# Group-query attention: the score products that only serve the row maxima, computed from the high parts alone and two heads at a time

## The chip, the cores and the metric

One core of a Trainium2 chip runs the whole program. The metric is the device time of one execution in microseconds (us); lower is better. A comparison of this kernel with itself settles at about 0.3%, some 5 us.

## What is computed

Two layers of a transformer trunk over 1024 latent and 256 context tokens. The change lies in the first layer, in its group-query attention (GQA): eight query heads of width 64 share two key and value heads. Cut to what matters:

```python
qb = rms_norm(qb.reshape(bsz, t, GQA_HEADS, GQA_HEAD_DIM), q_norm_b)      # 8 heads of 64
kb = rms_norm(kb.reshape(bsz, t, GQA_KV_HEADS, GQA_HEAD_DIM), k_norm_b)   # 2 heads of 64
qb = apply_axial_rope(qb, rope_b); kb = apply_axial_rope(kb, rope_b)      # latents only
sc = jnp.einsum('bqhgd,bkhd->bhgqk', qblk, k) * scale                     # over context + latent keys
p = jax.nn.softmax(sc, axis=-1)
ob = jnp.einsum('bhgqk,bkhd->bqhgd', p, v)
```

Beside GQA the layer has eight heads of latent attention (MLA) with products of 96 rows, which run after the GQA heads through the same code. The second layer is recurrent and not touched.

## The kernel before

Every fp32 operand is split into a high part, rounded to the fast fp32r type, and a low part, the remainder. A query vector q is stored as high and low rows of one 128-row tile (`qh`: rows 0 to 63 high, 64 to 127 low); for keys the tile `kh` has the high part in both halves, and `kl` has the low part and rows of ones.

Attention is cut into 16 units: 8 of GQA (`kind` "g"), then 8 of MLA. A unit is two heads (`j` = 0, 1) and either 768 queries (512 latents and the 256 context tokens) or the other 512 latents. A unit's softmax needs, ahead of its scores, the largest score of every query. `prep_max` makes these: for each head, each tile of 128 queries and each stretch of keys (512, 512, 256) a product with the query tile as weights goes to one PSUM bank (`ps`), and VectorE reduces it to a maximum (`mx`). For GQA this product contracts all 128 rows, (high + low of q) times high of k. The maxima, negated and as two bf16 terms (`nb`), are transposed by four small products against an identity (`bias`, `identbf` in the rows) and copied by ScalarE into two spare rows of `ql`, so that the second score product subtracts them.

`scores` then makes, for each block of 128 keys, two products per head (`pb` tiles, the second with 66 rows of `ql`), and ScalarE takes the exponential. `values` multiplies by v, with the two heads in the two column halves of the array (`pv`). An iteration of the main loop is one block of keys: scores of head 0, a call of `between`, scores of head 1, another `between`; the products of `values` follow every second iteration. `between` advances the preparation of the next unit by `pace` pieces, a piece being one step of `prep_max`. The orders of TensorE and VectorE in this loop are those of the program text; ScalarE's is the scheduler's. Units 0 and 1 are prepared earlier, during the projections, where four pieces are taken at each step, and where products for the modulation (`modw`, four in four column quarters) are interleaved too. In the attention loop the PSUM tag `ps` has 4 banks, `pb` 3 and `pv` 1; during the projections `ps` has all 8.

`post_q` lays out the query tiles that `prep_q_gqa` later loads into `qh` and `ql`. All matrix and elementwise calls go through helpers, so the profile shows line 88 for all of them; tiles tell them apart.

Of the kernel before, what the change touches and what calls it, by code (L numbers as in the profile page):

```python
# [17 lines left out]
P = 128  # L18
# [93 lines left out]
class Trunk:  # L112
# [202 lines left out]
    def project0(self, er, el, att):  # L315
        tc, nc, I, d = self.tc, self.nc, self.I, self.d
# [170 lines left out]
        for c, (t0, n) in enumerate(CH):  # L487
            rk = self.til(wk1, [P, 4, 128], F32, "rawA")
            for i in range(n // P):
                t = t0 // P + i  # L490
# [8 lines left out]
        def post_q(t, acc):  # L499
            raw4 = acc.rearrange("p (t h e) -> p t h e", t=1, e=64)  # L500
            qn = self.norm_rope(wk, raw4, raw4, 1, 8, rope_q, t, "g")[:, 0]
            q2 = self.til(wk, [P, 8, 2, 64], F32R, "q2", bufs=3)
            nc.scalar.activation(q2[:, :, 0], qn, AF.Copy)
            nc.vector.tensor_tensor(q2[:, :, 1], qn, q2[:, :, 0], op=ALU.subtract)

            def pe():
                for g in range(2):
                    qo = self.til(wk, [P, 4, P], F32R, "qo", bufs=3)
                    pq = self.ps([P, 4, P])
                    for j in range(4):  # L510
                        self.tr(pq[:, j], q2[:, 4 * g + j].rearrange("p a b -> p (a b)").bitcast(F32))
                    nc.scalar.activation(qo, pq, AF.Copy)
                    nc.sync.dma_start(d["q12"][t, :, 4 * g:4 * g + 4], qo.bitcast(F32))

            self.defer(3, pe)
# [78 lines left out]
    def attention(self, es):  # L594
# [81 lines left out]
        def prep_q_gqa(u):  # L676
            q_tiles(u)
            p = u["p"]
            a = u["base"] // P
            n = sum(x[1] for x in u["segs"])  # L680
            for j in range(2):
                src = d["q12"][a:a + n // P, :, 2 * p + j, :].rearrange("t p n -> p t n")
                nc.sync.dma_start(u["qh"].bitcast(F32)[:, j, :n].rearrange("p (t n) -> p t n", n=P), src)
                nc.sync.dma_start(u["ql"].bitcast(F32)[0:64, j, :n].rearrange("p (t n) -> p t n", n=P), src[0:64])
            u["k"] = [gk[p // 2], gk[p // 2]]
            yield

# [45 lines left out]

        def prep_max(u):

            K, r0 = (P, 64) if u["kind"] == "g" else (96, 96)
            mt = u["ql"] if u["kind"] == "g" else u["qh"]
            mx = self.til(u0, [P, 8, 3], F32, "mx", bufs=2)
            m8 = self.til(u0, [P, 2, 6, 2], F32, "m8", bufs=2)
# [9 lines left out]
            for t0, n in u["segs"]:  # L749
                if t0 == 0:  # L750
                    yield "late"
                ksegs = [(0, 256)] if t0 == 0 else [(0, 512), (512, 512), (1024, 256)]
                o = (t0 - u["base"]) // P
                nt = n // P
                for j in range(2):
                    kh = u["k"][j][0]
                    for i in range(nt):
                        for g, (s0, sn) in enumerate(ksegs):
                            sp = self.ps([P, 512])
                            self.mm(sp[:, :sn], u["qh"][0:K, j, (o + i) * P:(o + i + 1) * P], kh[0:K, s0:s0 + sn], True, True)  # L760
                            dst = m8[:, j, o + i, 0:1] if t0 == 0 else mx[:, 4 * j + i, g:g + 1]
                            nc.vector.tensor_reduce(dst, sp[:, :sn], axis=AX.X, op=ALU.max, negate=t0 == 0)
                            yield 0
                            if t0 and j and (i, g) == (1, 2):
                                bias(0, t0, n)
                    oo = slice(o, o + nt)
                    red = nc.vector.tensor_reduce
                    if t0:
                        red(m8[:, j, oo, 0], mx[:, 4 * j:4 * j + 4], axis=AX.X, op=ALU.max, negate=True)
                    red(nb[:, j, oo, 0], m8[:, j, oo, 0:1], axis=AX.X, op=ALU.max)  # L770
                    red(m8[:, j, oo, 1], nb[:, j, oo, 0:1], axis=AX.X, op=ALU.max, negate=True)
                    with self.tc.nc.allow_low_precision(reason="the second of two bf16 terms of a maximum"):
                        red(nb[:, j, oo, 1], m8[:, j, oo], axis=AX.X, op=ALU.add)
                yield 3
                if t0 == 0:
                    bias(0, t0, n)
                bias(1, t0, n)

# [196 lines left out]
        for i, it in enumerate(its):  # L975
            ui = it["ui"]
            if ui != cur:
                cur = ui
                if ui + 1 < len(units):
                    nu = units[ui + 1]  # L980
                    if nu["kind"] == "m" and side:
                        for _ in side[0]:
                            pass
                        side = []
                    gens.append([nu["gen"], 0, False])
                    pieces = 25 + (0 if nu["kind"] == "g" else 5 if nu["base"] == 0 else 1)
                    pace = pieces / 14.0 if nu["base"] == 0 else (pieces + 4) / 16.0
            if it["last"] and ui + 1 < len(units):
                while gens and not gens[0][2]:
                    advance(gens[0], True)  # L990
# [1250 lines left out]
```

## Time and profile before

| | before |
|---|---|
| median of 3 runs | 1787.96 us (1785.87 to 1790.78) |
| the profiled execution, its time | 1786.52 us |
| the profiled execution, its span | 1784.7 us |
| TensorE busy | 1630.5 us, 91% |
| VectorE busy | 1177.7 us, 66% |
| ScalarE busy | 741.0 us, 42% |
| GpSimd busy | 811.2 us, 45% |
| granted TensorE clock, mean | 0.96 |

The span is that of the recorded instructions; 1.8 us of the execution lie around it. The GQA units run from about 355 to 612 us of the span, the MLA units after them to about 920 us, and the projections, with the preparation of units 0 and 1, before them.

### The profile page before, as it was taken

To read this page: it belongs to the slowest core of one execution; us is meant where nothing else is said; L and a number is where in the kernel's file an instruction comes from. 1 tells how busy PE (TensorE), PEld (TensorE's weight loads), DVE (VectorE), ACT (ScalarE), POOL (GpSimd) and SP (SyncE) were. 2 spreads that over 40 slices of the span, in tenths; PEclk is the share of its full clock that TensorE was granted. 3 is DMA by queue.
4 is the path that set the end of the run, shared out by engine and by line. 5 is a ranking of instruction groups with operands and counts; after the bars stand their busy time and mean duration, and the time that the engine had idled before them with its cause. 6 is when DMAs were issued, how large, how long until landed. Compare 5 with 4: busy or idle time off the path is not lost.

```text
span 1784.7 us, 25505 instructions
## 1 busy us (share of the span) xinstructions
PE 1630.5 (91%) x9020; PEld 1195.9 (67%) x9020; DVE 1177.7 (66%) x2186; ACT 741.0 (42%) x1500; POOL 811.2 (45%) x727
## 2 busy tenths in 40 slices
PE   5999899989999999999899989988978995898996
PEld 2997766735555566666457876666856883798885
DVE  2657623247566857667847975889956894477787
ACT  2543401145545454444524344767643421233431
POOL 1432200067666678767643851332213794572131
PEclk9999999999999999999999999989989997899998
DMA  9243485164322101121333323333458538985543
GB/s 354 75 154 109 147 292 201 60 142 144 94 53 59 35 22 47 30 59 48 98 98 113 130 91 102 111 107 115 145 140 213 159 115 233 295 259 174 172 147 106
DMA packets 239931, 234.31 MB, mean 131 GB/s; under 512 B 61958, under 2 KB 188306, under 8 KB 237756
## 3 DMA queue, kind: packets, MB, share of 16 engines
q1 hardware_dynamic: 239804, 232.69, 42.8%
q8 instruction: 71, 1.16, 0.3%
q14 instruction: 56, 0.46, 0.1%
HBM read 162.97 MB, written 69.66 MB: 130 GB/s over the span
## 4 chain that ended last, share of the span: by engine, by line
PE 51%; DVE 18%; DMA 13%; issue 7%; ACT 6%; POOL 3%; SPq 2%; ACTq 0%; DVEq 0%; POOLq 0%
PE ps L88 34%; PE pb L88 10%; PE pv L88 7%; DMA wst<-in_att_w_in 2%; DVE f L88 2%; DMA wh<-in_rec_w_out 2%; DVE x L88 2%; DVE yc L88 2%; DVE lw L88 1%; DVE mx L88 1%; DMA qh<-d_q 1%; DMA d_xa<-WX 1%; DVE WX L88 1%; DVE r L88 1%; DVE lu L88 1%
## 5 line engine op out<-in xcount | busy, mean ns | idle before, releaser
L88 DVE TENSOR_REDUCE mx<-ps 128x1 f32<-128x512 f32 (+1 forms) x384 | 207.2, 593 | 155.8 <-PE ps L88 154.1
L88 POOL TENSOR_TENSOR accp<-accp,pt 128x512 f32<-128x512 f32 x202 | 266.0, 1338 | 62.0 <-ACT pt L88 60.4
L88 PE MATMUL ps<-h1h,wf 128*128 128x512 f32 (+1 forms) x864 | 270.5, 388 | 3.5 <-DVE tm L88 1.6
L88 ACT ACTIVATE pt<-pb 128x512 f32<-128x512 f32 (+1 forms) x352 | 194.2, 577 | 185.7 <-PE pb L88 178.0
L88 PE MATMUL pb<-qh,kb 96*128 96x512 f32 (+4 forms) x528 | 210.0, 412 | 5.2 <-ACT pt L88 4.6
L88 PEld LDWEIGHTS ps<-h1h,wf 128*128 128x128 f32 x864 | 161.1, 194 | 35.4 <-issue 3.7
L88 PE MATMUL ps<-h1l,wf 128*128 128x512 f32 (+1 forms) x432 | 163.7, 379 | 0.0
L88 PEld LDWEIGHTS pb<-qh,kb 128*128 128x128 f32 (+2 forms) x528 | 100.1, 191 | 92.6 <-issue 65.4
L88 PE MATMUL pb<-ql,kb 66*128 66x512 f32 (+3 forms) x352 | 137.5, 392 | 0.7 <-ACT ql L88 0.7
L88 PE MATMUL ps<-kb,qh 128*128 128x512 f32 (+3 forms) x416 | 121.7, 368 | 8.9 <-DVE mx L88 5.0
L88 POOL TENSOR_TENSOR accp<-pt,pt 128x512 f32<-128x512 f32 (+1 forms) x47 | 55.9, 1208 | 137.0 <-ACT pt L88 125.3
L88 PEld LDWEIGHTS ps<-kb,qh 128*128 128x128 f32 (+1 forms) x416 | 76.9, 191 | 44.8 <-DVE mx L88 12.8
L88 POOL TENSOR_TENSOR ml<-m,mh 128x512 fp32r<-128x512 f32 (+1 forms) x24 | 52.6, 2205 | 114.0 <-ACT mh L88 114.0
L88 DVE SCALAR_TENSOR_TENSOR yc<-xb,rT,yc 128x1283 f32<-128x1283 f32 (+1 forms) x48 | 84.1, 1759 | 24.5 <-ACT yc L88 24.1
L88 PEld LDWEIGHTS ps<-h1l,wf 128*128 128x128 f32 x432 | 83.9, 194 | 16.6 <-issue 3.6
L88 PE MATMUL ps<-w,mh 128*128 128x512 f32 x256 | 82.5, 404 | 3.4 <-ACT mh L88 3.4
L88 PE MATMUL pv<-pt,vm 128*64 128x512 f32 (+1 forms) x352 | 83.1, 586 | 1.6 <-DVE mo L88 1.6
L88 PE MATMUL pv<-pt,vgqa 128*64 128x512 f32 (+1 forms) x352 | 83.1, 593 | 1.0 <-DVE mo L88 1.0
L88 PE MATMUL ps<-wo,mh 128*128 128x512 f32 x256 | 82.1, 399 | 1.2 <-ACT mh L88 0.7
L88 PE MATMUL ps<-wh,hh 128*128 128x416 f32 (+2 forms) x240 | 82.8, 349 | 0.2 <-ACT hs L88 0.2
L88 PE MATMUL ps<-wh,hl 128*128 128x416 f32 (+2 forms) x240 | 81.7, 343 | 0.0
L88 PE MATMUL ps<-wl,hh 128*128 128x416 f32 (+2 forms) x240 | 81.5, 342 | 0.0
(373 smaller groups left out, 3706.0 us busy)
## 6 DMA issues: line engine op xcount, KB each, us to landing
modw<-in_mod_w SPq DMA_DIRECT2D x16, 1024.0 KB
wfs<-in_rec_w_in SPq DMA_DIRECT2D x22, 512.0 KB
modw<-in_mod_w SPq DMA_DIRECT2D x16, 512.0 KB
wst<-in_att_w_in SPq DMA_DIRECT2D x24, 256.0 KB
d_q<-qo SPq DMA_DIRECT2D x20, 256.0 KB
lx<-d_xl SPq DMA_DIRECT2D x8, 640.0 KB
d_w<-WX SPq DMA_DIRECT2D x20, 256.0 KB
W<-d_w SPq DMA_DIRECT2D x20, 256.0 KB
```

The source lines that it names most:

```text
L88: return fn(*args, **kw)
```

## The change

Three things. First, the layout: for odd heads `post_q` now stores low rows above and high rows below, so that the high parts of head 0 lie in rows 0 to 63 and those of head 1 in rows 64 to 127 of a unit's `qh`; the `ql` load follows this. Second, for GQA `prep_max` contracts only 64 rows (high of q times high of k), and one piece makes the products of both heads, in the two row halves of the array, into two `ps` banks, followed by two reductions. The maximum is thus taken over slightly different scores; it is only the shift of the softmax and cancels in the result. Third, what depends on the pieces: a GQA unit counts 13 pieces instead of 25, with paces of 13/15 and 15/18 of a piece per `between` instead of 25/14 and 29/16, and the two `bias` groups of a segment both come at its end, where before the first came in the middle of head 1. MLA keeps its order.

```diff
-            nc.scalar.activation(q2[:, :, 0], qn, AF.Copy)
-            nc.vector.tensor_tensor(q2[:, :, 1], qn, q2[:, :, 0], op=ALU.subtract)
+            qp, q4 = qn.rearrange("p (g e) n -> p g e n", e=2), q2.rearrange("p (g e) a n -> p g (e a) n", e=2)
+            nc.scalar.activation(q4[:, :, 0::3], qp, AF.Copy)
+            nc.vector.tensor_tensor(q4[:, :, 1:3], qp, q4[:, :, 0::3], op=ALU.subtract)
...
-                nc.sync.dma_start(u["ql"].bitcast(F32)[0:64, j, :n].rearrange("p (t n) -> p t n", n=P), src[0:64])
+                nc.sync.dma_start(u["ql"].bitcast(F32)[0:64, j, :n].rearrange("p (t n) -> p t n", n=P), src[64 * j:64 * j + 64])
...
-                for j in range(2):
-                    kh = u["k"][j][0]
+                pair = u["kind"] == "g"
+                for js in ((0, 1),) if pair else ((0,), (1,)):
                     for i in range(nt):
                         for g, (s0, sn) in enumerate(ksegs):
-                            sp = self.ps([P, 512])
-                            self.mm(sp[:, :sn], u["qh"][0:K, j, (o + i) * P:(o + i + 1) * P], kh[0:K, s0:s0 + sn], True, True)
-                            dst = m8[:, j, o + i, 0:1] if t0 == 0 else mx[:, 4 * j + i, g:g + 1]
-                            nc.vector.tensor_reduce(dst, sp[:, :sn], axis=AX.X, op=ALU.max, negate=t0 == 0)
+                            sps = [self.ps([P, 512]) for _ in js]
+                            for j, sp in zip(js, sps):
+                                r = slice(64 * j, 64 * j + 64) if pair else slice(0, 96)
+                                self.mm(sp[:, :sn], u["qh"][r, j, (o + i) * P:(o + i + 1) * P], u["k"][j][0][r, s0:s0 + sn], True, True)
+                            for j, sp in zip(js, sps):
+                                dst = m8[:, j, o + i, 0:1] if t0 == 0 else mx[:, 4 * j + i, g:g + 1]
+                                red(dst, sp[:, :sn], axis=AX.X, op=ALU.max, negate=t0 == 0)
                             yield 0
-                            if t0 and j and (i, g) == (1, 2):
+                            if t0 and js == (1,) and (i, g) == (1, 2):
                                 bias(0, t0, n)
...
                 yield 3
-                if t0 == 0:
+                if t0 == 0 or pair:
                     bias(0, t0, n)
                 bias(1, t0, n)
...
-                    pieces = 25 + (0 if nu["kind"] == "g" else 5 if nu["base"] == 0 else 1)
-                    pace = pieces / 14.0 if nu["base"] == 0 else (pieces + 4) / 16.0
+                    pieces = 13 if nu["kind"] == "g" else 25 + ( 5 if nu["base"] == 0 else 1)
+                    if nu["base"] == 0:
+                        pace = pieces / (15.0 if nu["kind"] == "g" else 14.0)
+                    else:
+                        pace = (pieces + (2 if nu["kind"] == "g" else 4)) / (18.0 if nu["kind"] == "g" else 16.0)
```

How the order moves, at three places. First TensorE in the middle of a GQA unit, where `pb` are scores of the running unit, `ps<-kb,qh` products for the maxima of the next one, and the last numbers partitions and columns of the output. Before:

```order
L88 MATMUL pb_4534<-qh_4157,kb_3304 128x512
L88 MATMUL pb_4534<-ql_4158,kb_3306 128x512
L88 MATMUL ps_4539<-kb_3304,qh_4482 128x512
L88 MATMUL ps_4542<-kb_3304,qh_4482 128x256
L88 MATMUL pb_4545<-qh_4157,kb_3304 128x512
L88 MATMUL pb_4545<-ql_4158,kb_3306 128x512
L88 MATMUL ps_4550<-kb_3304,qh_4482 128x512
L88 MATMUL ps_4553<-kb_3304,qh_4482 128x512
```

and now:

```order
L88 MATMUL pb_4609<-qh_4157,kb_3304 128x512
L88 MATMUL pb_4609<-ql_4158,kb_3306 128x512
L88 MATMUL ps_4614<-kb_3304,qh_4495 128x512
L88 MATMUL ps_4615<-kb_3304,qh_4495 128x512
L88 MATMUL pb_4620<-qh_4157,kb_3304 128x512
L88 MATMUL pb_4620<-ql_4158,kb_3306 128x512
L88 MATMUL pv_4513<-pt_4543,vgqa_102 64x512
L88 MATMUL pv_4513<-pt_4557,vgqa_102 64x512
```

Two consecutive `ps` products were two pieces of one head; now they are one pair, one in rows 0 to 63 and one in rows 64 to 127, between score products that use all rows. In the GQA loop there are 78 pairs: 61 (40 of 512 columns, 21 of 256) stand between products in the full 128 by 128 shape, 17 (8 of 512, 9 of 256) have `values` products behind them.

Second, TensorE and ScalarE where a new unit begins (its tiles are `qh_4157` and `ql_4158`). TensorE before:

```order
L88 LDWEIGHTS nb_4177
L88 MATMUL ps_4428<-identbf_83,nb_4177 2x128
L88 MATMUL pb_4434<-qh_4157,kb_3304 128x512
L88 MATMUL pb_4434<-ql_4158,kb_3306 128x512
L88 MATMUL ps_4439<-kb_3304,qh_4157 128x256
L88 MATMUL ps_4442<-kb_3304,qh_4157 128x256
L88 MATMUL pb_4445<-qh_4157,kb_3304 128x512
L88 MATMUL pb_4445<-ql_4158,kb_3306 128x512
```

and now:

```order
L88 LDWEIGHTS nb_4182
L88 MATMUL ps_4422<-identbf_83,nb_4182 2x128
L88 LDWEIGHTS nb_4182
L88 MATMUL ps_4428<-identbf_83,nb_4182 2x128
L88 LDWEIGHTS nb_4182
L88 MATMUL ps_4428<-identbf_83,nb_4182 2x128
L88 LDWEIGHTS nb_4182
L88 MATMUL ps_4428<-identbf_83,nb_4182 2x128
L88 LDWEIGHTS nb_4182
L88 MATMUL ps_4428<-identbf_83,nb_4182 2x128
L88 MATMUL pb_4434<-qh_4157,kb_3304 128x512
L88 MATMUL pb_4434<-ql_4158,kb_3306 128x512
```

ScalarE there before:

```order
L88 ACTIVATE ql_4158<-ps_4354 2x512
L88 ACTIVATE pt_4369<-pb_4366 128x512
L88 ACTIVATE pt_4387<-pb_4384 128x512
L88 ACTIVATE pt_4398<-pb_4395 128x512
L88 COPY vm_4100<-ps_4405 128x512
L88 ACTIVATE pt_4419<-pb_4416 128x512
L88 ACTIVATE pt_4424<-pb_4421 128x512
L88 ACTIVATE ql_4158<-ps_4428 2x512
L88 ACTIVATE pt_4437<-pb_4434 128x512
```

and now:

```order
L88 ACTIVATE pt_4405<-pb_4402 128x512
L88 ACTIVATE pt_4418<-pb_4415 128x512
L88 ACTIVATE ql_4158<-ps_4422 2x512
L88 ACTIVATE ql_4158<-ps_4428 2x512
L88 ACTIVATE pt_4437<-pb_4434 128x512
```

The bias of head 0 (`ps_4354`) was copied six ScalarE instructions ahead of that of head 1; now both copies stand right ahead of the unit's first scores, and eight small products stand in a row where four stood. This is so at all six borders between GQA units whose preparation runs in the loop.

Third, TensorE in the projections, at the preparation of unit 1. Before, `modw` products came four in a row:

```order
L88 MATMUL ps_2802<-modw_2857,scT_78 32x512 x4
L88 MATMUL ps_3012<-kb_2300,qh_2868 128x512
L88 MATMUL ps_3015<-kb_2300,qh_2868 128x256
L88 MATMUL ps_3022<-kb_2300,qh_2868 128x512
L88 MATMUL ps_3025<-kb_2300,qh_2868 128x512
```

and now:

```order
L88 MATMUL ps_2882<-modw_2826,scT_78 32x512 x2
L88 MATMUL ps_2897<-kb_2300,qh_2678 128x512
L88 MATMUL ps_2902<-kb_2300,qh_2678 128x512
L88 MATMUL ps_2882<-modw_2826,scT_78 32x512 x2
L88 MATMUL ps_2903<-kb_2300,qh_2678 128x512
```

Four `modw` groups of four stand in eight separate places now, with products for the maxima between, and four of the 26 pairs there (three of 512 columns, one of 256) are themselves parted. Counted over the order, TensorE's shape (rows by columns of the array that a product uses) changes 119 times in the GQA loop before and 248 times now, and 36 and 54 times in the projections.

## Rows read from the trace of the kernel before

**Rows 1.** The page, part 1: busy us, share of the span, instructions.

```profile
PE 1630.5 (91%) x9020; PEld 1195.9 (67%) x9020; DVE 1177.7 (66%) x2186; ACT 741.0 (42%) x1500; POOL 811.2 (45%) x727
```

**Rows 2.** Busy us by stretch: PE, PEld, DVE, ACT, POOL, then PE's clock, DMA share, GB/s.

```profile
233.00:355.00 122.00, 115.47 (x643) 85.93 (x642) 34.31 (x84) 16.10 (x30) 4.14 (x3) 1.00 0.54 177
420.00:460.00 40.00, 39.06 (x177) 21.18 (x175) 29.08 (x58) 21.95 (x42) 29.26 (x24) 1.00 0.29 72
```

**Rows 3.** Waits from 420 to 580 us: who for whom, total us, times, longest.

```profile
DVE mx L88 <- PE ps L88: 36.4, 23, 3.2
...
PE ps L88 <- DVE mx L88: 1.0, 3, 0.6
```

**Rows 4.** Timeline of PE, 377.7 to 384.3 us: start, duration, instruction, count.

```profile
377.79 0.28 PE L88 MATMUL pb<-ql,kb 66*128 66x256 f32 x1
...
378.03 0.29 PE L88 MATMUL pb<-ql,kb 66*128 66x256 f32 x1
...
378.95 0.40 PE L88 MATMUL pb<-ql,kb 66*128 66x512 f32 x1
379.28 1.08 PE L88 MATMUL pv<-pt,vgqa 128*64 128x256 f32 x8
...
382.89 0.40 PE L88 MATMUL pb<-ql,kb 66*128 66x512 f32 x1
...
383.83 0.40 PE L88 MATMUL pb<-ql,kb 66*128 66x512 f32 x1
```

**Rows 5.** Timeline of PE around a product of 16 rows, in the second layer.

```profile
1334.50 0.39 PE L88 MATMUL ps<-maskr,negi 128*128 128x512 f32 x1
1334.82 0.49 PE L88 MATMUL ps<-dec 16*128 16x512 f32 x1
1335.24 0.50 PE L88 MATMUL ps<-h1l,wf 128*128 128x512 f32 x1
1335.58 0.63 PE L88 MATMUL ps<-h1h,wf 128*128 128x512 f32 x2
```

**Rows 6.** PE's timeline and group: fp32 products in rows 0-31 and 32-63 (count | busy, mean ns).

```profile
934.57 0.70 PE L88 MATMUL ps<-grows,sel 32*128 32x512 f32 x2
...
L88 PE MATMUL ps<-grows,sel 32*128 32x512 f32 x4 | 1.1, 640 | 0.0
```

**Rows 7.** Timeline of PE where a new GQA unit begins, from 479 us.

```profile
479.11 0.40 PE L88 MATMUL pb<-ql,kb 66*128 66x512 f32 x1
479.44 0.38 PE L88 MATMUL ps<-identbf,nb 128*2 128x128 bf16 x4
479.76 0.50 PE L88 MATMUL pb<-qh,kb 128*128 128x512 f32 x1
480.10 0.40 PE L88 MATMUL pb<-ql,kb 66*128 66x512 f32 x1
...
480.56 0.39 PE L88 MATMUL pb<-qh,kb 128*128 128x512 f32 x1
480.88 0.50 PE L88 MATMUL pb<-ql,kb 66*128 66x512 f32 x1
```

**Rows 8.** Timeline of ACT there, and at the unit begin near 445 us.

```profile
479.13 1.08 ACT L88 ACTIVATE pt<-pb 128x512 f32<-128x512 f32 x2 [2.01 <-PE pb L88]
480.24 0.59 ACT L88 ACTIVATE ql<-ps 2x512 fp32r<-2x512 f32 x1
...
445.44 0.59 ACT L88 ACTIVATE ql<-ps 2x512 fp32r<-2x512 f32 x1
```

**Rows 9.** Timeline of PE in the projections, around a group of modw products.

```profile
277.75 1.06 PE L88 MATMUL ps<-modw,scT 128*32 128x512 f32 x8
278.74 0.38 PE L88 MATMUL ps<-kb,qh 128*128 128x256 f32 x1
```

**Rows 10.** Groups by form: of 420 to 580 us, then of 140 to 200 us (query layout).

```profile
L88 DVE TENSOR_REDUCE mx<-ps 128x1 f32<-128x512 f32 x80 | 52.5, 681 | 28.3 <-PE ps L88 28.3
...
L88 DVE TENSOR_TENSOR q<-no,q 128x512 fp32r<-128x512 f32 x9 | 6.2, 687 | 4.0 <-ACT q L88 4.0
```

More of the change, by code (lines that the diff above doesn't have):

```diff
@@ L734, in prep_max @@
         def prep_max(u):
-            K, r0 = (P, 64) if u["kind"] == "g" else (96, 96)
+            r0 = 64 if u["kind"] == "g" else 96
             mt = u["ql"] if u["kind"] == "g" else u["qh"]
@@ L754, in prep_max @@
                 nt = n // P
-                for j in range(2):
-                    kh = u["k"][j][0]
+                red = nc.vector.tensor_reduce
+                oo = slice(o, o + nt)
+                pair = u["kind"] == "g"
+                for js in ((0, 1),) if pair else ((0,), (1,)):
                     for i in range(nt):
                         for g, (s0, sn) in enumerate(ksegs):
-                            sp = self.ps([P, 512])
-                            self.mm(sp[:, :sn], u["qh"][0:K, j, (o + i) * P:(o + i + 1) * P], kh[0:K, s0:s0 + sn], True, True)
-                            dst = m8[:, j, o + i, 0:1] if t0 == 0 else mx[:, 4 * j + i, g:g + 1]
-                            nc.vector.tensor_reduce(dst, sp[:, :sn], axis=AX.X, op=ALU.max, negate=t0 == 0)
+                            sps = [self.ps([P, 512]) for _ in js]
[5 more added lines that the diff above has]
+                                red(dst, sp[:, :sn], axis=AX.X, op=ALU.max, negate=t0 == 0)
@@ L763, in prep_max @@
                             yield 0
-                            if t0 and j and (i, g) == (1, 2):
+                            if t0 and js == (1,) and (i, g) == (1, 2):
                                 bias(0, t0, n)
[L766 to L770, printed above, removed]
@@ L771, in prep_max @@
-                    red(m8[:, j, oo, 1], nb[:, j, oo, 0:1], axis=AX.X, op=ALU.max, negate=True)
-                    with self.tc.nc.allow_low_precision(reason="the second of two bf16 terms of a maximum"):
-                        red(nb[:, j, oo, 1], m8[:, j, oo], axis=AX.X, op=ALU.add)
+                    for j in js:
+                        if t0:
+                            red(m8[:, j, oo, 0], mx[:, 4 * j:4 * j + 4], axis=AX.X, op=ALU.max, negate=True)
+                        red(nb[:, j, oo, 0], m8[:, j, oo, 0:1], axis=AX.X, op=ALU.max)
+                        red(m8[:, j, oo, 1], nb[:, j, oo, 0:1], axis=AX.X, op=ALU.max, negate=True)
+                        with self.tc.nc.allow_low_precision(reason="the second of two bf16 terms of a maximum"):
+                            red(nb[:, j, oo, 1], m8[:, j, oo], axis=AX.X, op=ALU.add)
```

## The prediction

> **What bounds the kernel now.** I read the page's busy shares first: TensorE is busy 91% of the span [rows 1]. Then the stretches in which the changed products run. In the GQA loop TensorE is busy 39.1 of 40 us at full clock, VectorE 29.1, ScalarE 22.0, GpSimd 29.3; in the projections it is busy 115.5 of 122 us [rows 2]. Then the waits: over 160 us of the loop VectorE waits 36.4 us for these products, and TensorE waits 1.0 us for VectorE's reductions [rows 3]. So TensorE sets the time there, and a microsecond more or less on its queue is one in the result. What counts on that queue is the step from one start to the next, not the shown durations, since products overlap. In a run of one shape a 512-column product takes a step of 0.235 us (four steps from 382.89 to 383.83) and a 256-column one 0.12 (two steps from 377.79 to 378.03) [rows 4].
>
> **What a pair saves.** A piece now makes two products in different row halves. Nothing before does this with fp32r in halves of 64. The nearest row is the pair of fp32 products in rows 0-31 and 32-63: records of 0.64 us each, two of them within 0.70 us and four within 1.1, so they run two at a time [rows 6]. The other bound is that they run one after the other, at 0.235 or 0.12 each [rows 4]. I take "together", because the neighbour differs only in the type and the height of the strips. A pair then saves one step.
>
> **What a pair costs.** The order puts nearly every pair between products of another shape, and a change of shape has a price in the trace. Around the 16-row product (fp32r, 512 columns, like ours) the steps are 0.32, 0.42 and 0.34 us [rows 5], where three steps within one shape are 0.705 [rows 4]: going in and out costs 0.375. The same is seen at column strips: 0.33 from a score product to `pv` [rows 4], 0.33, 0.32 and 0.34 around the bias products [rows 7]. No row shows the shape 64 by 128. Bounds: nothing, if a change between 128 and 64 rows were free, and 0.375. I take 0.375, since all neighbours, taller and shorter, pay it.
>
> The Trainium skill, in "TensorEngine Tiling (Array Packing)", section "Key Properties", says that changing the tiling mode, not just the tile, drains TensorE. It gives no price. By that rule rows 5 are the general case, and it speaks against this change.
>
> **The sum in the GQA loop.** Four steps from the product ahead of a pair to the second behind it:
> - 61 pairs between full-shape products. 512 columns: before 4 x 0.235 = 0.94, after 0.32 + 0.42 + 0.34 = 1.08, so +0.14 each, 40 of them: +5.6 us. 256 columns: before 0.235 + 0.12 + 0.12 + 0.235 = 0.71, after 1.08 less the 0.115 that the shorter stream saves = 0.965, so +0.255, 21 of them: +5.4.
> - 17 pairs with `pv` behind them, where a change of shape was paid already (0.33). 512: before 0.235 + 0.235 + 0.33 = 0.80, after 0.32 + 0.42 = 0.74, -0.06 each, 8 of them: -0.5. 256: before 0.235 + 0.12 + 0.215 = 0.57, after 0.625, +0.055, 9 of them: +0.5.
>
> Together +11.0 us. Put differently: 48 + 30 steps saved are 11.3 + 3.6 = 14.9 us, 139 added changes of shape at 0.1875 are 26.
>
> **Bias.** A group of four costs 0.33 + 0.32 + 0.34 - 0.47 = 0.52 us [rows 7]. Four more in the same shape add the 0.32 less the 0.10 by which a first product after a change is late, 0.22. Merging saves 0.30, six times: -1.8. But the copy of head 0's bias into `ql` now stands right ahead of the unit's first scores. At 479 us ScalarE was held by exponentials until 480.24 and copied until 480.83 [rows 8]; the second score product that needed this copy began at 480.88 [rows 7]. Now that slot belongs to head 0, whose second score product would be due at 480.10 + 0.22 = 480.32, and head 1's copy ends 0.59 later: waits of 0.57 and 0.11 us, against 0.085 before (480.88 less 480.56 and a step), so +0.6. Behind the short context units ScalarE copies from 445.44 [rows 8], some 0.4 sooner: about +0.3. What is queued behind the waiting product is the whole TensorE queue, `pv` of the old unit included. Three borders of each kind: +2.7. Bounds: 0, and 0.7 at each with a second copy's wait of 0.6: 8.
>
> **Projections.** 22 of the 26 pairs stay together (13 of 512, 9 of 256): -13 x 0.235 - 9 x 0.12 = -4.1 us. 18 more changes of shape: +3.4. Four `modw` groups stand in eight places; a part lasts as long as a whole group of four, 0.99 us to the next product less 0.14 for the change [rows 9], so 4 x 0.85 = +3.4. Eight reductions per step instead of four are 5.4 us of VectorE at 0.68 [rows 10] in a step of 24 products x 0.235 = 5.6: just covered, and I add 0.3 for the bank waits at the beginning of a burst. Sum +3.0, range -4 to +8.
>
> **At nothing.** `post_q`'s copy and subtraction handle the same 512 elements per row (the subtraction 0.69 us [rows 10], ten of each) in other places; they are waited for by transposes three tiles later, and ScalarE and VectorE have room. Were the cover gone and each 0.1 longer, 2 us. The `ql` loads have the same size and place on SP's queue. In the loop the number of reductions is unchanged; a pair needs two of four `ps` banks, which I price at 0, at most at 4 us (78 x 0.05).
>
> Sum: +11.0 - 1.8 + 2.7 + 3.0 = +14.9, say +15 on the profiled execution's 1786.5 (span 1784.7 and 1.8 around it), 1801.5. The median of the runs is 1.4 above that execution: 1788 + 15 = **1803 us**.
>
> **Rivals.**
> - Faster: the change between 128 and 64 rows is free, and the pairs overlap. Place: the 78 + 22 pairs. Then the loop gains 14.9 + 1.8 - 2.7 and the projections 4.1 - 3.4: -15, **1773 us**. It decides from a price of 14.7 / 157 = 0.094 per change of shape, half of the measured one. For it: the trace has no 64 by 128 product. Against it: rows 5, and also fp32 strips pay.
> - The page "TensorE: Matmul & The Clock Gate" of the Trainium skill, section "Measured speedup vs the span model", prices a packed group at one product plus about 4 ns per tile and nothing for going in and out. By that rule alone this rival holds.
> - The change doesn't do what it says: the halves take turns. Then 61 steps of 0.235 (48 + 13) and 39 of 0.12 come on top, 14.3 + 4.7 = 19: **1822 us**. For it: no fp32r product in a strip has a partner in this trace. Against it: rows 6.
> - About even: one of the two switches is hidden, say because the pair's weights are loaded while the old shape still runs, so that a change costs 0.09 to 0.11: **1788 us**, within 0.3%. Against it: in rows 5 both ways show, 0.085 going in and 0.29 behind it.
>
> **How the numbers follow.** Forecast 0.60, turns 0.12, even 0.14, free 0.14. The forecast's own range is 1795 to 1812 (projections -4 to +8, border waits 0 to 8, taken together). For 8 in 10 the range must hold the even case too and reach into the case of turns: 1784 to 1820, which leaves out the free case and some of the turns. A measurement of this kernel tells about 0.3%, 5 us, from no change: slower 0.70 (the forecast nearly whole, and the turns), same 0.15, faster 0.15.
>
> **What would show it.** In the trace of the changed kernel: steps of about 0.32 into a pair and 0.42 out of it, with 0.34 behind, in the GQA loop; the two records of a pair starting together; the GQA loop longer by some 12 us, TensorE still busy in nearly all of it; a wait of TensorE for ScalarE's `ql` at each of six unit borders; MLA and the second layer as before. Steps of 0.235 around a pair would make the forecast wrong and the free case right; second products one step behind the first would show the turns; a TensorE that waits for VectorE's reductions would show a bound that I priced at nothing.

## The result, and the profile after

The changed kernel takes **1809.3 us** (median of 4 runs, 1807.24 to 1815.81) against 1789.3 for the kernel before beside it: ratio 1.0112, 95% interval 1.0088 to 1.0136. It is slower by 20 us; forecast were 15 more. A second comparison gave 1811.3, ratio 1.0120 (1.0076 to 1.0165). The profiled execution is the slowest of the first four (1815.81 us, span 1814.0).

Part 1 of its page, which answers to [rows 1]:

```profile
PE 1654.5 (91%) x9020; PEld 1187.7 (65%) x9020; DVE 1171.1 (65%) x2186; ACT 740.5 (41%) x1500; POOL 814.3 (45%) x727
```

TensorE has the same number of products and 24 us more of busy time. Where they lie is seen when the span is cut at the first product for the maxima, the first `pb` and the last `pv` of GQA and of MLA. Columns as in [rows 2]; the rows are the projections, the GQA loop and MLA. The kernel before:

```profile
241.64:355.56 113.92, 109.30 (x605) 82.95 (x605) 34.31 (x84) 15.50 (x29) 4.14 (x3) 1.00 0.49 163
355.56:612.47 256.91, 241.93 (x1069) 131.02 (x1067) 162.71 (x335) 127.78 (x239) 174.71 (x142) 0.98 0.34 90
612.47:913.75 301.28, 295.62 (x1341) 178.65 (x1337) 207.82 (x382) 143.06 (x260) 214.33 (x167) 0.99 0.18 50
```

and the changed kernel:

```profile
241.69:362.91 121.22, 115.26 (x605) 82.54 (x605) 33.30 (x84) 15.33 (x29) 3.88 (x3) 0.97 0.46 152
362.91:639.26 276.35, 258.86 (x1068) 120.43 (x1067) 160.05 (x335) 127.72 (x239) 173.39 (x142) 0.95 0.32 84
639.26:940.55 301.29, 295.38 (x1341) 178.88 (x1337) 207.83 (x382) 143.15 (x260) 214.52 (x167) 0.99 0.18 50
```

The projections are 7.3 us longer, the GQA loop 19.4, MLA not at all. Two columns differ beside the length: idle time (length less the first busy column) is 17.5 instead of 15.0 us in the loop, and the mean clock is 0.95 instead of 0.98.

The pairs themselves, in TensorE's timeline, which answers to [rows 4]:

```profile
469.30 0.50 PE L88 MATMUL pb<-qh,kb 128*128 128x512 f32 x1
469.63 0.40 PE L88 MATMUL pb<-ql,kb 66*128 66x512 f32 x1
469.96 0.50 PE L88 MATMUL ps<-kb,qh 64*128 64x512 f32 x2
470.39 0.50 PE L88 MATMUL pb<-qh,kb 128*128 128x512 f32 x1
470.73 0.40 PE L88 MATMUL pb<-ql,kb 66*128 66x512 f32 x1
```

A step of 0.33 us into the pair, 0.43 out of it and 0.34 behind. The pair is one row of 0.50 us, as long as one product: its two records start 2 to 5 ns apart.

A border between units, which answers to [rows 7]; TensorE, then VectorE:

```profile
527.02 0.28 PE L88 MATMUL pb<-ql,kb 66*128 66x256 f32 x1
528.97 0.41 PE L88 MATMUL ps<-identbf,nb 128*2 128x128 bf16 x4 [1.66 <-DVE nb L88]
529.62 0.59 PE L88 MATMUL ps<-identbf,nb 128*2 128x128 bf16 x4 [0.26 <-DVE nb L88]
530.14 0.80 PE L88 MATMUL pb<-qh,kb 128*128 128x512 f32 x1
530.74 0.63 PE L88 MATMUL pb<-ql,kb 66*128 66x512 f32 x1
531.16 0.63 PE L88 MATMUL pb<-qh,kb 128*128 128x512 f32 x1
...
536.45 0.40 PE L88 MATMUL pb<-qh,kb 128*128 128x512 f32 x1
536.69 0.39 PE L88 MATMUL pb<-ql,kb 66*128 66x512 f32 x1
```

```profile
524.51 1.94 DVE L88 TENSOR_REDUCE mx<-ps 128x1 f32<-128x512 f32 x4
526.37 0.68 DVE L88 TENSOR_TENSOR accv<-accv,pt 128x512 f32<-128x512 f32 x1
526.97 0.68 DVE L88 TENSOR_TENSOR mo<-mo,rc 128x512 f32<-128x512 f32 x1
527.57 0.68 DVE L88 TENSOR_TENSOR mo<-pv,gt 128x512 f32<-128x512 f32 x1
528.17 0.15 DVE L88 TENSOR_REDUCE m<-mx 128x4 f32<-128x12 f32 x1
...
528.75 0.16 DVE L88 TENSOR_REDUCE nb<-m 128x4 bf16<-128x8 f32 x1
```

The last maxima are there at 526.45, but in VectorE's order an addition and two multiplications of the old unit stand ahead of the small reductions that make the bias terms. TensorE waits 1.66 us for `nb`. Behind the wait it runs at the lower of its two clock levels (1.2 instead of 2.4 GHz) from 529.20 to 536.03: steps of 0.60 and 0.42 where 0.34 and 0.235 are usual, so about 0.44 of the time is lost.

The longer waits of TensorE from 355 to 640 us (total us, times, longest), which answer to [rows 3]:

```profile
PE ps L88 <- DVE nb L88: 4.9, 6, 1.7
PE ps L88 <- DVE mx L88: 4.1, 2, 3.3
PE pb L88 <- ACT pt L88: 2.6, 2, 1.4
...
PE pb L88 <- ACT ql L88: 1.1, 3, 0.4
PE ps L88 <- DMA qh<-d_q: 1.1, 1, 1.1
```

and the first four of these in the kernel before:

```profile
PE ps L88 <- DVE mx L88: 5.1, 5, 3.3
PE pb L88 <- ACT pt L88: 4.6, 2, 3.3
...
PE pb L88 <- ACT ql L88: 0.7, 1, 0.7
PE ps L88 <- DVE nb L88: 0.3, 2, 0.2
```

The waits for `nb` are 4.6 us longer, but those for `pt` and `mx` 3.0 us shorter, and with the smaller ones the idle time in all grew by 2.5 us only.

### The profile page after: what moved, and what is told of

Read it like the earlier page. It is cut to its first block, busy times and chain, and to the rows that moved or that the text cites. A ratio compares the mean times of both kernels' runs of the same rounds, so it can differ in the third digit from the quotient of the medians.

```text
span 1814.0 us, 25501 instructions
## 1 busy us (share of the span) xinstructions
PE 1654.5 (91%) x9020; PEld 1187.7 (65%) x9020; DVE 1171.1 (65%) x2186; ACT 740.5 (41%) x1500; POOL 814.3 (45%) x727
## 4 chain that ended last, share of the span: by engine, by line
PE 52%; DVE 19%; DMA 10%; issue 7%; ACT 6%; POOL 3%; SPq 2%; DVEq 0%; ACTq 0%; POOLq 0%
PE ps L88 34%; PE pb L88 10%; PE pv L88 7%; DVE f L88 2%; DVE yc L88 2%; DVE mx L88 2%; DVE x L88 2%; DMA modw<-in_mod_w 1%; DVE lw L88 1%; DVE ia L88 1%; DVE r L88 1%; DMA wh<-in_rec_w_out 1%; DVE lu L88 1%; ACT lw L88 1%; POOL lu L88 1%
## 5 line engine op out<-in xcount | busy, mean ns | idle before, releaser
L88 PE MATMUL pb<-qh,kb 96*128 96x512 f32 (+4 forms) x528 | 217.1, 425 | 3.7 <-ACT pt L88 3.2
L88 PE MATMUL ps<-kb,qh 64*128 64x512 f32 (+3 forms) x416 | 109.6, 407 | 9.8 <-DMA qh<-d_q 4.7
L88 PEld LDWEIGHTS ps<-kb,qh 64*128 64x128 f32 (+1 forms) x416 | 60.2, 189 | 62.1 <-issue 25.1
L88 PEld LDWEIGHTS ps<-h1l,wf 128*128 128x128 f32 x432 | 84.8, 196 | 16.2 <-issue 3.3
L88 POOL TENSOR_TENSOR wl<-wst,wh 128x512 fp32r<-128x512 f32 (+2 forms) x20 | 24.8, 1243 | 132.5 <-ACT wh L88 132.3
```

What stands on the lines that cost most here:

```text
L88: return fn(*args, **kw)
```

## The experiments

Each loop below is split in three: TensorE's idle time; what the low clock cost (0.44 of the time at the low level outside of waits, from the records of the granted clock); and the rest, which is the steps. The three columns are those of one profiled execution; the clock's part varies most from one to the next. The medians are of 4 runs, of 10 for the order alone. Over the 92 executions of these kernels, each compared with the others of its own kernel, the time goes up by about 0.95 us where the mean clock of TensorE falls by 0.001; that accounts for some four tenths of the spread. One profiled execution can lie over 10 us off its kernel's median, and the row of the kernel before rests on one execution too.

| kernel | median us | ratio, 95% | shape changes in loop | loop | idle | low clock | steps |
|---|---|---|---|---|---|---|---|
| before | 1786.5 to 1791.5 | | 119 | 256.9 | 15.0 | 3.8 | 238.1 |
| changed | 1809.3 | 1.0088 to 1.0136 | 248 | 276.4 | 17.5 | 11.2 | 247.7 |
| changed, again | 1811.3 | 1.0076 to 1.0165 | 248 | 277.3 | 19.7 | 8.9 | 248.6 |
| 64 rows alone | 1815.4 | 1.0100 to 1.0177 | 266 | 280.1 | 11.4 | 5.7 | 263.0 |
| order alone | 1806.8 | 1.0059 to 1.0109 | 109 | 260.2 | 19.1 | 6.0 | 235.1 |
| earlier pieces | 1816.4 | 1.0113 to 1.0175 | 243 | 279.7 | 16.9 | 15.2 | 247.6 |
| queries first | 1809.9 | 1.0094 to 1.0151 | 248 | 273.7 | 18.0 | 8.2 | 247.5 |
| projections as before | 1810.6 | 1.0087 to 1.0156 | 248 | 277.7 | 19.8 | 9.5 | 248.4 |
| two pairs | 1820.1 | 1.0141 to 1.0212 | 178 | 283.0 | 25.1 | 15.5 | 242.4 |
| all three | 1814.8 | 1.0122 to 1.0182 | 178 | 283.2 | 25.5 | 13.9 | 243.8 |
| pairs, fewer waits | 1801.2 | 1.0055 to 1.0098 | 243 | 270.7 | 12.6 | 8.8 | 249.3 |
| full rows, fewer waits | 1797.8 | 1.0045 to 1.0080 | 109 | 263.2 | 16.9 | 7.0 | 239.3 |
| before, late bias | 1834.5 | 1.0234 to 1.0289 | 119 | 302.8 | 48.4 | 16.2 | 238.2 |
| pairs, direct terms | 1805.7 | 1.0088 to 1.0155 | 245 | 270.1 | 13.7 | 8.6 | 247.8 |

Theory S puts the loss on the changes of shape, theory O on the order of the pieces and the waits that it makes. Theory W, in the later experiments, puts what the steps don't explain on single waits of TensorE and on the low clock behind them; each expectation says which waits it means.

**Changed again.** 

> The changed kernel once more, for a second profile: 1807 to 1816 us, steps of 0.33, 0.43 and 0.34 us around a pair, TensorE's waits for nb at the borders and a half clock behind two of them if these belong to the kernel and not to one execution.

It came out at 1811.3. The steps around a pair are the same, and the waits for `nb` are too (5.2 us, the two longest 1.66 and 1.67). The half clock behind these two is not the same. At the first of them:

```profile
529.84 0.38 PE L88 MATMUL ps<-identbf,nb 128*2 128x128 bf16 x4 [1.66 <-DVE nb L88]
...
530.81 0.50 PE L88 MATMUL pb<-qh,kb 128*128 128x512 f32 x1
531.15 0.40 PE L88 MATMUL pb<-ql,kb 66*128 66x512 f32 x1
531.39 0.40 PE L88 MATMUL pb<-qh,kb 128*128 128x512 f32 x1
```

Steps of 0.34 and 0.24 us, the full level, where the first execution had 6.8 us at the low one; behind the second wait are 3.4 us of it. So the waits belong to the kernel. The low clock behind waits of this length belongs to the execution: this part of the expectation failed.

**64 rows alone.** The kernel before with one word changed, so that every product for the maxima contracts the high rows only, one after the other:

```diff
-            K, r0 = (P, 64) if u["kind"] == "g" else (96, 96)
+            K, r0 = (64, 64) if u["kind"] == "g" else (96, 96)
```

> The kernel before with one thing changed: the GQA products for the maxima contract the 64 high rows only, still one head after the other and in the same order, so no two of them can overlap. Theory S (the loss is the price of changes of shape, 0.1875 us each): the order has 266 changes in the GQA loop against 119, and 53 against 36 in the projections, 164 more x 0.1875 = +31 us, 1820 us, with steps of 0.32 into and 0.42 out of a group of 64-row products. Theory O (the loss comes from moved pieces, loads and bias copies): nothing is moved here, so the time of before, 1789 us. If 64 rows were as cheap to enter as 128, also 1789 us.

Measured: +24 us. The steps of the loop grow by 24.9 us over 147 more changes of shape: 0.17 us each (forecast 0.1875). S holds in kind, somewhat below its 31 us. TensorE's timeline:

```profile
471.05 0.73 PE L88 MATMUL ps<-kb,qh 64*128 64x512 f32 x2
471.70 0.96 PE L88 MATMUL ps<-wukv,ck 128*128 128x512 f32 x3
```

Two such products and the way out take 0.65 us; one takes 0.42. So a second product of half the rows costs 0.23 us, a step as with all rows, and going in and out costs 0.34 us (twice 0.17). The low clock cost 5.7 us here, where it cost 3.8 before and 8.9 to 11.2 with the change: products of 64 rows alone didn't bring in this execution what the change brought in its two.

**The order alone.** The changed kernel's pieces, places and paces with the old layout and all 128 rows:

```diff
-                                r = slice(64 * j, 64 * j + 64) if pair else slice(0, 96)
+                                r = slice(0, P) if pair else slice(0, 96)
```

> The changed kernel with its order, pieces, paces and bias places, but the old layout and products that contract all 128 rows, so that the two products of a piece take turns in the full shape. Theory S: merging the bias groups gains 1.8 us, the copies into ql at six borders cost 2.7, and what the profile of the changed kernel shows beside that (TensorE waits 4.9 us for VectorE's bias terms at the borders, where it waited 0.3 us before, and runs at half clock for 6.8 us after two of them) some 7 more: 1795 to 1799 us, with 109 changes of shape in the GQA loop. Theory O: the whole loss is here, 1809 us.

Measured 1806.8: O is nearer. The order without a pair costs some 15 us, and the pairs then add 2.5 to 4.5 us by the medians (5 to 6.5 by the ratios), known to about 5 us. The steps of the loop are 3.0 us shorter, where the merged bias groups were to give 1.8; idle time, the clock and the projections (121.1 us) are longer. The profiled execution is the fastest of the ten (1795.3, 8.8 us above that of the kernel before), so the table shows less than the median holds, and some 6 of the 15 us are in no profile.

**Earlier pieces.** The changed kernel with paces of 13/12 and 15/14, so that the maxima are done well ahead of the border:

```diff
-                        pace = pieces / (15.0 if nu["kind"] == "g" else 14.0)
+                        pace = pieces / (12.0 if nu["kind"] == "g" else 14.0)
...
-                        pace = (pieces + (2 if nu["kind"] == "g" else 4)) / (18.0 if nu["kind"] == "g" else 16.0)
+                        pace = (pieces + (2 if nu["kind"] == "g" else 4)) / (14.0 if nu["kind"] == "g" else 16.0)
```

> The changed kernel with quicker paces for GQA (13/12 and 15/14 pieces per call in place of 13/15 and 15/18), so that VectorE's last small reductions come earlier than the bias products that wait for them. If the border waits and the half clock behind them are a part of the loss: 4 to 9 us less than the changed kernel, 1800 to 1805 us, and TensorE's wait for nb falls from 4.9 to under 1 us in the GQA loop. If they are not: 1809 us. Changes of shape stay (243 against 248 in the loop).

A miss: slower, not faster. The waits for `nb` are gone, but others stand in their place: 8.4 us for `qh` in the loop, where 1.1 stood. TensorE's timeline at one of them:

```profile
464.56 0.49 PE L88 MATMUL ps<-kb,qh 64*128 64x512 f32 x1
468.53 1.22 PE L88 MATMUL ps<-kb,qh 64*128 64x512 f32 x3 [3.48 <-DMA qh<-d_q]
```

The first product of the first pair runs, the second waits for the second head's `qh`, which before the change was needed twelve pieces later. Taken earlier, the pairs run into the load.

**Queries first.** The two `qh` loads ahead of the two `ql` loads:

```diff
-            for j in range(2):
-                src = d["q12"][a:a + n // P, :, 2 * p + j, :].rearrange("t p n -> p t n")
+            srcs = [d["q12"][a:a + n // P, :, 2 * p + j, :].rearrange("t p n -> p t n") for j in range(2)]
+            for j, src in enumerate(srcs):
                 nc.sync.dma_start(u["qh"].bitcast(F32)[:, j, :n].rearrange("p (t n) -> p t n", n=P), src)
+            for j, src in enumerate(srcs):
                 nc.sync.dma_start(u["ql"].bitcast(F32)[0:64, j, :n].rearrange("p (t n) -> p t n", n=P), src[64 * j:64 * j + 64])
```

> The changed kernel, but the two `qh` loads of a unit are issued ahead of its two `ql` loads, nothing else. Theory W: a pair needs the second head's `qh` at once, and the waits for that load (about 3.6 us in the projections and 1 to 4 us in the GQA loop, some with a stretch of low clock behind them) are part of the loss: these waits go, and the kernel takes 1803 to 1806. Theory S: what counts are the changes of shape alone, which stay at 248 and 55: 1810, as the changed kernel. Rival to both: the `ql` loads now land later and the first scores wait for them: slower than 1810.

Measured 1809.9, no change, where theory W had 1803 to 1806. But the edit took only part of the waits away. The loop's wait for `qh` is gone, though one of 1.5 us for `ql` stands there now, where the longest was 0.4; in the projections (120.5 us) the first pair still waits 2.0 us for its second `qh`. So theory W missed, and what a pair without that wait would gain is not shown.

**Projections as before.** Units 0 and 1 by single heads and full rows:

```diff
-                pair = u["kind"] == "g"
+                pair = u["kind"] == "g" and u["i"] > 1
+                K = P if u["kind"] == "g" else 96
...
-                                r = slice(64 * j, 64 * j + 64) if pair else slice(0, 96)
+                                r = slice(64 * j, 64 * j + 64) if pair else slice(0, K)
```

> The changed kernel, but units 0 and 1, which are prepared during the projections, are prepared as before the change: one head at a time, 128 rows, first bias group in the middle. Shape changes in the projections are 36 again, in the GQA loop 248. The projections were 7 us longer with the change, forecast were 3. If the pairs and the places of the modulation products there are the cause, the projections come back to about 114 us and the kernel to 1802 to 1804. If those 7 us come from something else that the profile shows there (the query layout, the loads), they stay: 1809 to 1811. The GQA loop is as in the changed kernel in either case, about 276 us.

In the profile the projections are back at 113.7 us with no low clock, as expected, and that execution took 1803.1. The median of the four is 1810.6 at a lower mean clock (0.951 against 0.954), so the time of the whole kernel doesn't show the gain. Inconclusive on the time, clear on the stage.

**Two pairs in a piece.** In the loop a piece is two pairs:

```diff
-                            yield 0
+                            if u["i"] < 2 or not pair or (i * len(ksegs) + g) % 2:
+                                yield 0
...
-                    pieces = 13 if nu["kind"] == "g" else 25 + ( 5 if nu["base"] == 0 else 1)
+                    pieces = 7 if nu["kind"] == "g" else 25 + ( 5 if nu["base"] == 0 else 1)
...
-                        pace = (pieces + (2 if nu["kind"] == "g" else 4)) / (18.0 if nu["kind"] == "g" else 16.0)
+                        pace = (pieces + (1 if nu["kind"] == "g" else 4)) / (18.0 if nu["kind"] == "g" else 16.0)
```

> The changed kernel, but in the GQA loop two pairs make one piece (four products in 64 rows in a row, four banks), at half the pace in pieces, so that the same work has 178 changes of shape instead of 248. Theory S (a change of shape costs 0.16 to 0.19 us): 70 x 0.16 to 0.19 is 11 to 13 us less, the loop near 264 us, the kernel 1797 to 1799, less if four products wait for banks. Theory O (the order of the pieces and waits at the unit borders cost most of it): the borders stay as they are, so 1808 to 1812, or slower because a group of four needs all four banks.

A miss for S: the slowest kernel with pairs. The steps fell by 5 to 6 us, not 11 to 13. Its timeline shows both sides, TensorE first, then VectorE:

```profile
484.59 0.40 PE L88 MATMUL pb<-ql,kb 66*128 66x512 f32 x1
484.92 0.62 PE L88 MATMUL ps<-kb,qh 64*128 64x512 f32 x4
485.47 0.50 PE L88 MATMUL pb<-qh,kb 128*128 128x512 f32 x1
485.81 0.40 PE L88 MATMUL pb<-ql,kb 66*128 66x512 f32 x1
...
486.62 1.33 PE L88 MATMUL ps<-kb,qh 64*128 64x512 f32 x4
487.88 0.50 PE L88 MATMUL pb<-qh,kb 128*128 128x512 f32 x1
```

```profile
485.45 1.95 DVE L88 TENSOR_REDUCE mx<-ps 128x1 f32<-128x512 f32 x4 [3.35 <-PE ps L88]
```

Where the four banks are free, four products and the way out take 0.55 us; the next group takes 1.26, since its second pair needs a bank that VectorE is still reducing (until about 487.3). At the borders the waits for `nb` grew to 2.7 us, three times, and the time at the low level in the loop to 44 us, from 27 and 20 in the two executions of the changed kernel.

**All three edits.** 

> The three edits of this call together: the two `qh` loads first, units 0 and 1 prepared as before the change, two pairs in a piece. If they add up (4 + 7 + 12 us, less 3 that the first two share) the kernel takes about 1790, as the kernel before; if the price of the shape is all that counts, 1791 to 1799 with the projections undone; if waits take the place of what is saved, above 1800.

They don't add up: 1814.8. The loop (283.2 us) is that of the two pairs (283.0).

**Pairs with fewer waits.** Queries first, projections as before and the earlier paces together. 

> The changed kernel with three edits meant to take its waits away: units 0 and 1 prepared as before the change, the two `qh` loads of a unit ahead of its `ql` loads, and paces of 13/12 and 15/14, so that the maxima are done earlier than the border of the unit. The pairs of the GQA loop stay: 243 changes of shape. Theory W (the loss beyond the steps is waits at the borders and for the second head's `qh`, and the low clock that follows a wait): the loop loses its waits of 1.7, 1.7 and 0.8 us for `nb`, its low clock falls from 27 to about 10 us as in the kernel before, the projections are 114 us, and the kernel takes 1797 to 1801, which is the price of the steps alone (+9 to +11). Theory P (the pairs themselves bring the low clock, by the load they put on the engine): the low clock stays above 20 us in the loop and the kernel takes 1804 to 1810.

Measured 1801.2, some 9 us below the changed kernel and at the upper edge of W. No wait for `nb` is left in the loop; two for `qh` (1.2 and 1.6 us) are. But low clock in the loop was 20.5 us, as much as in the second execution of the changed kernel and twice what W had; above 20 was the sign of theory P, whose time (1804 to 1810) missed. One stretch of it (from 439.4 us) has no wait over 0.25 us in the 8 us ahead. So neither theory holds whole.

**Full rows with fewer waits.** The same with 128 rows, `slice(0, P)`, in the loop. 

> The same kernel with one thing more: in the GQA loop the two products of a piece contract all 128 rows again, (high + low) times high, one after the other. So only the order, the merged bias groups and the loads differ from the kernel before; 109 changes of shape. Against the run with pairs this is the price of the pairs by itself. Theory S: 134 changes less at 0.16 to 0.19 (21 to 25 us less), 78 steps more (14.9 us more): 7 to 10 us less than the run with pairs, about 1789 to 1792. Theory W adds that the low clock in the loop is like that of the kernel before. If order alone, freed of these waits, still costs 9 us or more (1797 and above), theory W is wrong.

Measured 1797.8, above the 1789 to 1792 of S and W: a miss. It is also above 1797, the mark that was set beforehand, so theory W, as it was stated, is wrong. By the steps the pairs cost 249.3 - 239.3 = 10.0 us, as S has it (134 x 0.1875 - 14.9 = 10.2). By the loop it is 7.5, because the kernel without pairs waits 4.3 us more. By the medians it is 3.4; the profiled executions, 10.1 us apart, are the slowest of the one kernel and the fastest of the other, and don't show why. Against the kernel before, its loop is 6.3 us longer: 1.9 idle, 3.2 clock, 1.2 steps. The waits had moved, not gone: for `qh` 3.4 us in the loop where 0.8 stood. So a kernel without waits was not tried. At the low level it spends 17.1 us of its loop, without a pair: against theory P.

**Before, with a late bias.** Work for VectorE ahead of the bias terms, nothing else:

```diff
+                    if t0 and j and u["kind"] == "g" and u["i"] > 1:
+                        junk = self.til(u0, [P, 256], F32, "junk", bufs=1)
+                        nc.vector.memset(junk, 0.0)
+                        for _ in range(10):
+                            nc.vector.tensor_tensor(junk, junk, junk, op=ALU.add)
```

> The kernel before, with one thing added: ahead of the small reductions of the second head's bias terms in the six GQA units prepared in the loop, VectorE does a clearing and ten additions on a scratch tile of 256 columns (about 3.6 us), so that the bias products of TensorE come to wait for `nb` at the borders as they do in the changed kernel, with no pair, no new order and no other change. In the trace of the kernel before `nb` is ready some 2 us ahead of its product at the border near 479 us, so about 1.6 us of wait at each of three to six borders: 5 to 10 us. Theory W (a wait at a border is paid a second time by a stretch of low clock behind it): low clock of 3.4 to 6.8 us behind most of these waits, half of it lost, 5 to 15 us more in all: 1798 to 1812. Rival: the clock doesn't follow such waits, and only the waits themselves are paid: 1793 to 1798, low clock in the loop at about 10 us as before.

The scratch work took 6.5 us, not 3.6, so the waits are longer than planned. Loop window and waits, then TensorE at one border:

```profile
357.67:660.48 302.81, 254.38 (x1068) 136.52 (x1067) 193.80 (x401) 127.70 (x239) 173.46 (x142) 0.91 0.29 77
```

```profile
PE ps L88 <- DVE nb L88: 34.6, 6, 7.3
```

```profile
502.84 0.59 PE L88 MATMUL ps<-identbf,nb 128*2 128x128 bf16 x4 [4.50 <-DVE nb L88]
503.35 0.80 PE L88 MATMUL pb<-qh,kb 128*128 128x512 f32 x1
503.94 0.63 PE L88 MATMUL pb<-ql,kb 66*128 66x512 f32 x1
504.37 0.63 PE L88 MATMUL ps<-kb,qh 128*128 128x256 f32 x2
```

Six waits of 4.5 to 7.3 us, and at each of the six borders, where the kernel before has none, a stretch at the lower level of 6.8 to 10.2 us that begins inside the wait. The loop is 45.9 us longer: 33.4 idle, 12.4 clock, 0.1 steps. So a wait of this length at a border is paid more than once, with products of 128 rows and without a pair. The rival falls; that waits as short as 1.7 us do the same is not shown by this run, and the second execution of the changed kernel speaks against it.

**Direct terms.** Queries first, projections as before, and no pause between the last pair and the small reductions:

```diff
-                            yield 0
+                            if not pair or (i, g) != (nt - 1, len(ksegs) - 1):
+                                yield 0
```

> The changed kernel with units 0 and 1 prepared as before the change and the two `qh` loads first, and for the pairs of the loop the small reductions that make the bias terms follow the last maximum directly in VectorE's order, where in the changed kernel two additions and two multiplications of the old unit stand between. The paces stay those of the changed kernel, 245 changes of shape. Theory W: the waits of 1.66 us at two borders and 0.8 at a third fall below 0.5, the low clock behind them goes too, and the loop falls from 276 to about 268 us: the kernel takes 1796 to 1801. If the border waits are no matter, it takes what the changed kernel takes less the projections, 1803 to 1806.

In the profile the waits for `nb` are gone from the loop, which is 270.1 us (268 expected), and that execution took 1803.1. The median is 1805.7, in the range of the other answer. A new wait of 2.2 us stands in the loop (`pv` for `mo`, 528 us), with low clock from 527.3. So I take it as undecided.

No kernel tried beat the kernel before.

## Why the prediction was right, point by point

**What bounds the kernel** held: TensorE is busy 94% of the longer loop, and MLA takes 301.28 and 301.29 us. But the stretch from which the prediction read the bound (420 to 460 us) is a quiet one. Over the whole loop before, TensorE was idle for 15.0 us and at the low level for 10.2, most of it around this wait:

```profile
401.26 0.79 PE L88 MATMUL pb<-qh,kb 128*128 128x512 f32 x1 [3.33 <-ACT pt L88]
401.85 0.63 PE L88 MATMUL pb<-ql,kb 66*128 66x512 f32 x1
```

So waits with low clock behind them could be seen in the trace of the kernel before.

**The pair together** held: two records of a pair start 2 to 5 ns apart, one step saved. The Trainium skill, "TensorE: Matmul & The Clock Gate", section "Measured speedup vs the span model", gives one product and about 4 ns for each further tile; the trace agrees, at 64 rows and fp32r too. By that rule alone the free rival would have held; it fell by what going in and out costs.

**The price of the shape** held: 0.33, 0.43 and 0.34 us around a pair for 0.32, 0.42 and 0.34. The neighbouring rows, a strip of 16 rows [rows 5], gave the price for 64. The Trainium skill, in "TensorEngine Tiling (Array Packing)", section "Key Properties", says that changing the tiling mode drains TensorE. The trace agrees in so far as every change costs time. The price by the runs is 0.17 us per change (64 rows alone) to 0.20 (0.33 + 0.43 + 0.34 less 0.705, halved), where the prediction had 0.1875.

**The sum in the loop** held for the steps: +11.0 and -1.8 were forecast for steps and bias groups, +9.2; the steps grew by 9.6 and 10.5 in the two executions. The loop as a whole, forecast some 12 us longer, grew by 19.4 and 20.4, for the two reasons that follow.

**The waits at the unit borders** were named for the wrong waiter. Forecast were +2.7 us for ScalarE's copies into `ql`; those waits went from 0.7 to 1.1, three of them and not six. The waits for VectorE's `nb` went from 0.3 to 4.9. The step that failed is the price of nothing for VectorE in the loop: the prediction counted reductions and banks (the waits for banks, `mx`, did not grow: 5.1 and 4.1), not the place of the small reductions behind `accv` and `mo` in VectorE's order. Idle time in all grew by 2.5 and 4.7 us, near the 2.7 by chance.

**The clock** had no term, and it is the largest miss: 5.1 to 7.4 us in the loop and 2.1 to 2.4 in the projections. In the changed loop five stretches of low clock begin, each inside a wait of 1.4 to 3.3 us or within 1.2 us of its end; two such stretches stood in the loop before. In the second execution there are six, two of them with no wait over 0.8 us in the 8 us ahead, and one of the longest waits for `nb` has none behind it. So waits of 4.5 us and more brought low clock each time, as the late bias shows; for the short ones it is argued, not shown.

**The projections** were forecast at +3.0, range -4 to +8, and came at +7.3 and +6.9: steps +3.8 both times, idle and clock the rest. The step that failed is under "At nothing": it prices the `ql` loads at nothing for their size and place and has no term for `qh`. The pair needs the second head's `qh` sooner:

```profile
241.69 0.47 PE L88 MATMUL ps<-kb,qh 64*128 64x512 f32 x1 [1.23 <-DMA qh<-d_q]
244.50 1.40 PE L88 MATMUL ps<-kb,qh 64*128 64x512 f32 x5 [2.35 <-DMA qh<-d_q]
```

The second head's `qh` is 2.35 us late, and low clock lasts from 242.5 to 249.3. The order alone, without a pair, has projections of 121.1 us too, and with units 0 and 1 as before they are 113.7: it is the new order there that costs.

Taken together in the profiled execution: steps +9.6, idle +2.5, clock +7.4, projections +7.3, or 26.8 us in these two stages; the medians differ by 20 to 22. The second execution shows 27.3 in the two stages, less 3.4 in the stretch ahead of them, in which the change touches only the query layout, and which begins the projections at 238.2 to 242.7 us over all runs. In these executions the steps of the loop came as forecast, and what is missing from the forecast is the clock in the loop and some 4 us in the projections.

Whole runs share the loss out otherwise, and by them the total was in part luck. The terms that have nothing to do with the pairs (-1.8, +2.7, +3.4 and +0.3) come to +4.6 in the forecast; the order alone costs some 15 us. The pairs' own terms (+11.0, -4.1 and +3.4) come to +10.3; by the medians the pairs add 2.5 to 4.5 us to the order, and 3.4 in the kernels with fewer waits. So the order was priced too low and the pairs too high, and the two errors partly cancel. That the pairs' steps cost what was forecast is shown in the traces; why so little of it reaches the median is not.

**The rivals.** Free change of shape, half hidden (about even), halves in turns: the steps into and out of a pair rule out the first two, the 2 to 5 ns between its records the third.

**What stays open:** where the 15 us of the order alone and the last 10 us of the order with full rows and fewer waits come from (their profiled executions show 8.8 and 7.2 us over that of the kernel before, the latter 6.3 in the loop), and why low clock at times begins with no wait ahead of it, and at times does not follow one.

## What to carry to other kernels

Halves of the array that run together save a step, but each excursion into another shape costs about 0.34 to 0.40 us in and out, more than the 0.235 us of the step saved: pack only what can stand in long runs, and see first that there are banks for it. Two pairs in a row with free banks took 0.33 + 0.55 + 0.34 = 1.22 us in and out, where six steps in one shape are 1.41; no kernel here turned that into a gain. When pieces become fewer and need two inputs at once, look at what was hidden by their spacing: the load of the second input and the small operations of another engine behind the last piece. Where the clock falls around waits of TensorE, as at all six borders with the late bias, a wait that the sum carries at its own length is too cheap. And look at the whole time beside the profiled execution: here they disagree on what the pairs cost.

## What was not expected of the hardware

- With the late bias a wait of 4.5 to 7.3 us at a border brought 6.8 to 10.2 us at the lower clock level each time; over the loop 33.4 us of waits came with 12.4 us lost to the clock. In the changed kernel two waits of 1.66 and 1.67 us had 6.8 us of low clock behind each in one execution, none and 3.4 us in another.
- The mean clock explains some four tenths of the spread between executions of one kernel, over 92 of them: about 0.95 us for each 0.001.
- A packed pair of 512 columns had a record of 0.50 us, one product's; a group of two pairs with free banks took 0.55 us to the next product's start.
